# A hybrid transformer layer on one core: evacuations charged to the background steps' credit, the group norm's reciprocal root in three steps

## The chip, the cores and the metric

The kernel runs on one core of one Trainium2 chip. A core has a matrix engine (TensorE, PE in the profile), a vector engine (VectorE, DVE), an activation engine (ScalarE, ACT), a general engine (GpSimd, POOL) and a queue engine (SyncE, SP) that starts DMA transfers. Each engine works through its own list of instructions in order and waits on semaphores for the others. The metric is the time of one execution on the device in microseconds (us), the median of several runs.

## The reference

One layer of an encoder with three mixers side by side, then an MLP, for one sequence of 256 tokens with 2048 channels, all in float32. Cut to what matters here:

```python
u = rms_norm(x, norm_mix_pre)
proj = u @ w_in
sb, fox, rw, gates = split(proj)
y_a = stick_breaking_attention(sb)          # 4 heads x 128
y_b = forgetting_attention(fox)             # 4 heads x 128
y_c = rwkv7_time_mix(rw)                    # 16 heads x 64, 1024 channels
g_a, g_b, g_c = split(sigmoid(gates))       # 2048 channels each
m = g_a * (y_a @ w_branch_a) + g_b * (y_b @ w_branch_b) + g_c * (y_c @ w_branch_c)
x = x + rms_norm(m @ w_out, norm_mix_post)
x = x + rms_norm(square(relu(rms_norm(x, norm_mlp_pre) @ w_mlp_up)) @ w_mlp_down, norm_mlp_post)
```

The end of the RWKV mixer is a group norm over each head's 64 channels, and this is where the reciprocal root stands that the change takes apart:

```python
mean = jnp.mean(y, axis=-1, keepdims=True)
var = jnp.mean(jnp.square(y - mean), axis=-1, keepdims=True)
y = (y - mean) * rsqrt(var + 64e-5) * ln_w + ln_b
y = (y + sum(r * k * r_k) * v) * g
```

## The kernel before

**Weights as a stream.** All large weights are one stream of 128 x 1024 float32 tiles, read from memory in order into three buffers, `raw`. Each tile is split into two parts that together keep float32's precision: the high half `whi` (ScalarE, line L173) and the low half `wlo` (VectorE, L175, raw minus high). Three buffers of each exist, and the split runs one tile ahead of its use (`AHEAD` = 1). TensorE then needs, for each tile, eight matmuls of 512 columns with the high half and the equivalent of four with the low half. `gemm()` (L191, L195, L197) makes units of the first projections, `tok()` (L220, L235) computes token by channel and yields its two token tiles, whose product lies in a bank of PSUM, the buffer that matmuls write into.

**Mixers as background steps.** The small, latency-bound work of the three mixers runs between the large matmuls. It is one Python generator, `mixers()`: stick-breaking attention, forgetting attention, the RWKV's low-rank projections, then the RWKV mixer in two halves of eight heads, `rwkv_half(0)` and `rwkv_half(1)`. After each few large matmuls, `gemm()` and `tok()` call `tick(f)`. It adds `f * SHARE` to a credit, at most 1.5, counts a hold down by `f`, and while the hold is over and the credit is positive it takes steps from the generator:

```python
credit[0] = min(credit[0] + f * SHARE, 1.5)
hold[0] -= f
while hold[0] <= 0 and credit[0] > 0 and step():
    pass
```

`step()` subtracts from the credit what the step yielded. A plain number is a price. A `("stage", price, hold)` also ends the loop and sets the hold, so that the next step, which needs the result of this one, comes some large matmuls later. That fixes where the small matmuls stand on TensorE. The order on ScalarE, VectorE and GpSimd in this part of the kernel is chosen by the scheduler of the tile framework from the same program, by a model of its own; only TensorE keeps the written order there. From the first group of the output projection on, all engines keep the written order.

**The steps of one half of the RWKV mixer** that this text speaks of: the norm of the keys (L702 to L710), where ScalarE needs an activation table for Ln and another for Exp; `gates()` for each of four pairs of heads (L732 to L763), with the tanh gates on ScalarE, a scan along time on VectorE (L735), two exponentials on ScalarE that read it (L738, L739) and VectorE work that reads those (L744 to L763); four score matrices (L777 to L791); an inversion of triangular matrices by substitution on VectorE (L817 to L834), which ends in four 32 x 32 transposes and in matmuls of TensorE (L839); the recurrence over four chunks of 64 tokens, three stages each; and the group norm for two times two pairs (L917 to L946).

**The group norm** squares on ScalarE (L922), takes sums by matmul (L100, L101 in `heads()`), adds the epsilon on ScalarE (L935), and calls `rsqrt()` (L262): Ln and Exp(-0.5 x) on ScalarE, each with its table load (L265, L266), then one Newton step in four operations on VectorE (L267 to L270). All of it is one step of the generator, with a price of 2.2.

**The branches.** `branch()` (L1013) runs the products of the three mixers' outputs with their branch weights through `tok()`, for four groups of 512 channels. For each of the two token tiles VectorE evacuates PSUM: one operation for the first branch (L1017), two for the others (L1019, L1020). While the branches of the first two mixers run, `rwkv_half` is still taking steps.

Of the kernel before, what the change touches and what calls it, by code (L numbers as in the profile page):

```python
# [19 lines left out]
D = 2048  # L20
KT = 16
AHEAD = 1
SHARE = 0.82
HALF = 1024
EPS = 1e-6
CE = -0.5 * math.exp(-0.5)
# [26 lines left out]
def hybrid_block(ctx, tc, xt, x, gains, params, consts, lora, gup, wst, out):  # L53
# [12 lines left out]
    def nm(s):  # L66
        uid[0] += 1
        return f"{s}_{uid[0]}"
# [4 lines left out]
    def mps():  # L73
        return pm.tile([128, 512], F32, tag="mps", name=nm("mps"), bufs=4)
# [4 lines left out]
    def tmp(n=T):  # L79
        return tpool.tile([128, T], F32, tag="tmp", name=nm("tmp"), bufs=3)  # L80
# [5 lines left out]
    def C(name, r=slice(0, 128), lo=0, hi=None):  # L86
        c0, w = CC[name]
        hi = w if hi is None else hi
        if name == "ident":
            return ident[r, lo:hi]  # L90
        if c0 < NR + 128:
            return cr[r, c0 - 128 + lo:c0 - 128 + hi].bitcast(F32)
        return con[r, c0 - 128 - NR + lo:c0 - 128 - NR + hi]
# [17 lines left out]
    credit = [0.0]  # L111
# [25 lines left out]
    def tick(f=1.0):  # L137

        credit[0] = min(credit[0] + f * SHARE, 1.5)
        hold[0] -= f  # L140
# [119 lines left out]
            V.scalar_tensor_tensor(dst[:, T:], src, scale, dst[:, 0:T].bitcast(F32), ALU.mult, ALU.subtract)  # L260
            return ins

    def rsqrt(y, m, t):

        A.activation(t, m, AF.Ln)  # L265
        A.activation(y, t, AF.Exp, scale=-0.5)  # L266
        V.tensor_tensor(t, y, y, ALU.mult)  # L267
        V.tensor_tensor(t, t, m, ALU.mult)
        V.tensor_scalar(t, t, -0.5, 1.5, ALU.mult, ALU.add)
        V.tensor_tensor(y, y, t, ALU.mult)  # L270
# [6 lines left out]
    def g1(w=T):  # L277
        return rp.tile([128, T], F32, tag="g1", name=nm("g1"), bufs=21)
# [141 lines left out]
    rstd = rp.tile([128, T], F32, tag="cs", name="rstd1", bufs=1)  # L420
# [9 lines left out]
    def norm():  # L430
        ps = mps()
        for i in range(2):
            PE.matmul(ps[:, 0:T], C("ones"), A6[:, i, :], start=i == 0, stop=i == 1)
        ms, t = tmp(), tmp()
        V.tensor_scalar(ms, ps[:, 0:T], 1.0 / D, EPS, ALU.mult, ALU.add)
        rsqrt(rstd, ms, t)

    upk = [pk() for _ in range(KT)]

# [226 lines left out]
    def rwkv_half(hf):  # L666
# [30 lines left out]
        for i2, ps in enumerate(pss):  # L697
            ri = B6[:, 2 * i2:2 * i2 + 2, :]
            sc = B6[:, 4:6, :]
# [119 lines left out]
        for s in range(31):  # L819
            n, m = 31 - s, s + 1  # L820
# [35 lines left out]
        y = {p: g1() for p in PR}  # L856
# [55 lines left out]
        for i2 in range(2):  # L912
            gq = rp.tile([128, 3, 128], F32, tag="gup", name=nm("gup"), bufs=1)
            for i in range(2):
                cs = slice(128 * PR[2 * i2 + i], 128 * PR[2 * i2 + i] + 128)
                with tc.issue_after(behind[1].ins):
                    nc.scalar.dma_start(out=gq[:, i, :], in_=gup[0:128, cs])  # L917
                    nc.scalar.dma_start(out=gq[32 * i:32 * i + 32, 2, :], in_=gup[128:160, cs])
            B6 = rp.tile([128, 6, T], F32, tag="b6", name=nm("gn"), bufs=1)
            var, ri, sc = B6[:, 0:2, :], B6[:, 2:4, :], B6[:, 4:6, :]  # L920
            for i in range(2):
                A.activation(sc[:, i, :], y[PR[2 * i2 + i]], AF.Square)  # L922
            hi, lo = pair(), pair()
            A.activation(hi, sc, AF.Copy)
            V.tensor_tensor(lo, sc, hi.bitcast(F32), ALU.subtract)
            yield ("stage", 0.1, 2.5)
            ps = mps()
            heads(ps, hi, lo)
            psg = [mps(), mps()]
            for i in range(2):  # L930
                PE.matmul(psg[i][:, 0:T], gq[:, i, :], sy, start=True, stop=False)
            for i in range(2):
                r = slice(32 * i, 32 * i + 32)
                PE.matmul(psg[i][:, 0:T], gq[r, 2, :], sz[r], start=False, stop=True)
            A.activation(var, ps.rearrange("p (a b) -> p a b", a=2), AF.Identity, scale=1.0 / 64, bias=cst[:, 1:2])  # L935
            yield ("stage", 0.1, 0)
            rsqrt(ri, var, sc)
            yield 2.2
            for i in range(2):
                p = PR[2 * i2 + i]  # L940
                V.tensor_tensor(y[p], y[p], ri[:, i, :], ALU.mult)
                A.activation(y[p], y[p], AF.Identity, scale=P("lnw", p), bias=P("lnb", p))
                V.tensor_tensor(y[p], y[p], bon[p], ALU.add)
                V.tensor_tensor(y[p], psg[i][:, 0:T], y[p], ALU.mult)
                yc[p] = y[p]
                yield 1.1  # L946
# [22 lines left out]
    for br in ("sb", "fox"):  # L969
        for s in ("q", "k"):  # L970
# [3 lines left out]
            for h in range(4):  # L974
                ps = unit(upk)
                t = g1()
# [35 lines left out]
    def branch(ys, ths, m, first):  # L1012

        for tt, ps in enumerate(tok(ys)):
            th = ths[tt]
            if first:
                V.scalar_tensor_tensor(m[:, tt, :], th, 1.0, ps, ALU.add, ALU.mult)  # L1017
            else:
                V.scalar_tensor_tensor(th, th, 1.0, ps, ALU.add, ALU.mult)  # L1019
                V.tensor_tensor(m[:, tt, :], m[:, tt, :], th, ALU.add)  # L1020

    ms = []
    for g in range(4):
        m = rp.tile([128, 2, 512], F32, tag="m", name=nm("m"), bufs=4)
# [446 lines left out]
    first = [sum(SIZES[:q]) for q in range(len(SIZES) + 1)]  # L1471
# [178 lines left out]
```

## Time and profile before

| | us |
|---|---|
| median of three runs | 1511.27 |
| lowest and highest of them | 1511.23 and 1512.3 |
| the profiled execution | 1512.76 |
| its span, first to last instruction | 1510.9 |

The granted TensorE clock of the profiled execution is 0.998 of full speed.

In the profile's rows L12 is line 12 of the kernel. PE is a matmul on TensorE, PEld the load of its stationary operand. A row of the timeline gives start, duration, engine, line, operation, the tile written and the tile read, and how often; in square brackets stands how long the engine sat idle before it, and which instruction ended that. A row of the waits names who waited, for whom, the sum, how many times and the longest. A row of the windows gives the window, its length, the busy time of PE, PEld, DVE, ACT and POOL with the number of instructions, the granted clock, and the DMA engines' share and rate. A row of the chain of waits gives a start, a duration, an engine, a tile, a line and a count.

### The profile page before, as it was taken

What the parts mean: (1) busy time and instruction counts of PE and PEld (TensorE: products, weight loads), DVE (VectorE), ACT (ScalarE), POOL (GpSimd) and SP (SyncE); (2) the same over time, 40 slices, a digit from 0 to 9 for tenths busy, and PEclk for the clock granted to TensorE, in tenths of its full rate; (3) what the DMA queues carried; (4) which work ended last, traced back from release to release, by engine and by line L of the source; (5) the groups of instructions that cost most, each with busy time, mean ns of one, the idle gap of its engine ahead of it and who ended that gap; (6) DMA issues with size and microseconds to landing.
All of it is one profiled execution on the core that took longest, in us unless ns stands there. A gap on an engine that the chain in (4) does not pass through costs nothing.

```text
span 1510.9 us, 22695 instructions
## 1 busy us (share of the span) xinstructions
PE 1492.3 (99%) x8384; PEld 1252.7 (83%) x8384; DVE 1207.6 (80%) x1673; ACT 939.4 (62%) x1433; POOL 94.6 (6%) x151
## 2 busy tenths in 40 slices
PE   9999999999999999999999999999999999999997
PEld 7888888887787887778888988888888888888886
DVE  7875679895678896476656778999899989999996
ACT  7665677545676445564445767677667666766663
POOL 0031003000002000000000000000000000000000
PEclk9999999999999999999999999999999999999999
DMA  7645455455444455355675758879888888889874
GB/s 266 196 168 182 141 180 162 148 179 187 134 170 166 155 190 174 127 182 193 214 245 172 253 178 252 251 220 287 258 262 235 222 274 240 270 265 255 251 222 150
DMA packets 104687, 312.71 MB, mean 207 GB/s; under 512 B 10240, under 2 KB 12288, under 8 KB 104576
## 3 DMA queue, kind: packets, MB, share of 16 engines
q1 hardware_dynamic: 93968, 279.87, 55.1%
q0 software_dynamic: 8064, 29.36, 10.4%
q10 hardware_dynamic: 2544, 2.03, 0.5%
q8 instruction: 66, 1.08, 0.3%
q14 instruction: 45, 0.37, 0.1%
HBM read 279.77 MB, written 2.10 MB: 187 GB/s over the span
## 4 chain that ended last, share of the span: by engine, by line
PE 94%; DVE 2%; issue 1%; ACT 1%; DMA 1%; DVEq 0%; POOLq 0%; POOL 0%; ACTq 0%; SPq 0%
PE gps L235 26%; PE gps L191 23%; PE gps L195 13%; PE gps L220 7%; PE mps L1368 3%; PE mps L1370 3%; PE mps L1369 3%; PE gps L1370 2%; PE gps L1368 2%; PE gps L1369 2%; PE gps L197 2%; DVE wlo L175 1%; PE mps L777 1%; PE gps L1157 1%; DMA raw<-in_wst_dram 1%
## 5 line engine op out<-in xcount | busy, mean ns | idle before, releaser
L175 DVE TENSOR_TENSOR wlo<-raw,whi 128x1024 fp32r<-128x1024 f32 x576 | 697.0, 1220 | 160.5 <-ACT whi L173 149.2
L173 ACT ACTIVATE whi<-raw 128x1024 fp32r<-128x1024 f32 x576 | 603.9, 1057 | 251.9 <-PE gps L235 85.8
L191 PE MATMUL gps<-pk,whi 128*128 128x512 f32 x1479 | 375.3, 392 | 0.5 <-DVE tmp L1286 0.3
L191 PEld LDWEIGHTS gps<-pk,whi 128*128 128x128 f32 x1479 | 274.4, 188 | 56.1 <-ACT whi L173 0.9
L235 PE MATMUL gps<-whi,pk 128*128 128x512 f32 x1004 | 254.8, 393 | 1.4 <-ACT whi L173 1.3
L195 PEld LDWEIGHTS gps<-pk,wlo 128*128 128x128 f32 x1582 | 215.6, 190 | 15.2 <-DVE wlo L175 0.3
L235 PEld LDWEIGHTS gps<-whi,pk 128*128 128x128 f32 x1004 | 186.1, 188 | 42.6 <-ACT whi L173 2.2
L195 PE MATMUL gps<-pk,wlo 128*128 128x256 f32 x1582 | 221.0, 282 | 0.0
L235 PE MATMUL gps<-wlo,pk 128*128 128x512 f32 x502 | 137.8, 393 | 1.7 <-DVE wlo L175 1.7
L235 PEld LDWEIGHTS gps<-wlo,pk 128*128 128x128 f32 x502 | 93.2, 188 | 22.4 <-DVE wlo L175 2.9
L1368 PE MATMUL mps<-whi,fm 128*128 128x512 f32 x224 | 88.6, 396 | 1.9 <-ACT whi L173 1.7
L1285 ACT ACTIVATE tmp<-gps 128x256 f32<-128x256 f32 x64 | 24.6, 384 | 102.9 <-PE gps L197 101.0
L1369 PE MATMUL mps<-whi,fm 128*128 128x512 f32 x224 | 87.7, 392 | 0.0
L1370 PE MATMUL mps<-wlo,fm 128*128 128x512 f32 x224 | 87.4, 390 | 0.0
L1348 POOL DMA_DIRECT2D raw<-raw x56 | 48.8, 872 | 572.4 <-DVE raw L1345 271.9
L1345 DVE TENSOR_TENSOR raw<-raw,raw 128x1024 f32<-128x1024 f32 x56 | 68.4, 1221 | 0.8
L1368 PE MATMUL gps<-whi,fm 128*128 128x512 f32 x168 | 65.9, 392 | 0.0
L1370 PE MATMUL gps<-wlo,fm 128*128 128x512 f32 x168 | 65.8, 391 | 0.0
L1369 PE MATMUL gps<-whi,fm 128*128 128x512 f32 x168 | 65.5, 390 | 0.0
L220 PE MATMUL gps<-whi,pk 128*128 128x512 f32 x224 | 60.7, 393 | 0.0
L1368 PEld LDWEIGHTS mps<-whi,fm 128*128 128x128 f32 x224 | 42.4, 189 | 10.0 <-ACT whi L173 4.0
L1370 PEld LDWEIGHTS mps<-wlo,fm 128*128 128x128 f32 x224 | 42.1, 188 | 9.5
(346 smaller groups left out, 1725.1 us busy)
## 6 DMA issues: line engine op xcount, KB each, us to landing
raw<-in_wst_dram SPq DMA_DIRECT2D x516, 512.0 KB, 4.4
raw<-raw POOLq DMA_DIRECT2D x56, 512.0 KB, 7.3
x<-in_xt_dram SPq DMA_DIRECT2D x8, 256.0 KB, 6.8
x<-in_x_dram SPq DMA_DIRECT2D x8, 256.0 KB, 5.1
raw<-in_wst_dram SPq DMA_DIRECT2D x4, 256.0 KB, 4.8
g<-in_gains_dram SPq DMA_DIRECT2D x4, 256.0 KB, 5.0
pk<-in_gains_dram SPq DMA_DIRECT2D x4, 256.0 KB, 6.9
out_dram<-x SPq DMA_DIRECT2D x4, 256.0 KB, 2.8
```

The source lines that it names most:

```text
L173: A.activation(hi, raw, AF.Copy)
L175: low = lambda: V.tensor_tensor(lo, raw, hi.bitcast(F32), ALU.subtract)
L191: PE.matmul(ps, hi[:, i * 128:i * 128 + 128], pks[i], start=first and i == 0, stop=False)
L195: PE.matmul(ps[:, 0:T], lo[:, i * 128:i * 128 + 128], pks[i][:, 0:T], start=False, stop=False)
L197: PE.matmul(ps, hi[:, (n - 1) * 128:n * 128], pks[n - 1], start=False, stop=True)
L220: PE.matmul(ps[tt], pks[k][:, c:c + 128], w[:, (k - k0) * 512:(k - k0) * 512 + 512], start=k == 0 and part == 0 and w is hl[0], stop=w is ...
L235: PE.matmul(ps[tt], pks[k][:, c:c + 128], w[:, (k - k0) * 512:(k - k0) * 512 + 512], start=k == 0 and part == 0 and w is hl[0], stop=False)
L1345: V.tensor_tensor(R[d, a], R[d, a], R[d, b], ALU.add)
L1348: G.dma_start(out=R[d, a], in_=R[d, b], accum_op=ALU.add)
L1368: PE.matmul(Q[f], a, w, start=d == d0 and i == 0, stop=False)
L1369: PE.matmul(Q[f], b, w, start=False, stop=False)
L1370: PE.matmul(Q[f], a, wl, start=False, stop=d == dn and i == 1)
```

## The change

Three edits, all of which act on when the steps stand in the program.

- `SHARE`, the credit for a tick, goes from 0.82 to 0.88.
- `rsqrt()` is taken apart into a generator `power()` (Ln, a yield, Exp, a yield) and a function `newton()` (the four VectorE operations). The norm at the start of the kernel runs both through at once, as before. In the group norm each yield of `power()` becomes a stage with price 0.1 and hold 1, so that Ln, Exp and the Newton step are three steps.
- `branch()` subtracts 0.6 from the credit for a token tile of the first branch and 1.2 for one of the others, before its evacuation.

```diff
-SHARE = 0.82
+SHARE = 0.88
...
-    def rsqrt(y, m, t):
+    def power(y, m, t):
 
         A.activation(t, m, AF.Ln)
+        yield
         A.activation(y, t, AF.Exp, scale=-0.5)
+        yield
+
+    def newton(y, m, t):
+
         V.tensor_tensor(t, y, y, ALU.mult)
         V.tensor_tensor(t, t, m, ALU.mult)
         V.tensor_scalar(t, t, -0.5, 1.5, ALU.mult, ALU.add)
         V.tensor_tensor(y, y, t, ALU.mult)
...
-        rsqrt(rstd, ms, t)
+        for _ in power(rstd, ms, t):
+            pass
+        newton(rstd, ms, t)
...
             yield ("stage", 0.1, 0)
-            rsqrt(ri, var, sc)
+            for _ in power(ri, var, sc):
+                yield ("stage", 0.1, 1)
+            newton(ri, var, sc)
             yield 2.2
...
         for tt, ps in enumerate(tok(ys)):
             th = ths[tt]
+            credit[0] -= 0.6 if first else 1.2
             if first:
                 V.scalar_tensor_tensor(m[:, tt, :], th, 1.0, ps, ALU.add, ALU.mult)
             else:
```

The new lines move the numbers of the lines behind them: what was L702 to L763 is L709 to L770 in the changed kernel, L266 is L267, L942 is L951, L1008 is L1017, and L1019 and L1020 are L1029 and L1030. The numbers of instructions of each engine are the same before and after. Three places show how the order moves; the number at a row's start is its position in the engine's list, and the number behind a tile's name is its buffer's.

First ScalarE in the gate work of the first half, at about 229 us of the profile. Before:

```order
225 L702 ACT_TABLE_LOAD
226 L702 ACTIVATE b_376_2045<-sq_2185 128x512
227 L703 ACT_TABLE_LOAD
228 L703 ACTIVATE b_376_2045<-b_376_2045 128x512
229 L638 ACTIVATE tmp_2288<-gps_2210 128x256
230 L173 ACTIVATE whi_2332<-raw_2330 128x1024
231 L732 ACTIVATE lw_2274<-mps_2260,wah 128x256
232 L733 ACTIVATE tha_2276<-mps_2261,wah 128x256
233 L734 ACTIVATE lw_2274<-lw_2274,cst 128x256
234 L640 ACTIVATE zp_2290<-tmp_2289,par 128x256
235 L173 ACTIVATE whi_2369<-raw_2367 128x1024
236 L738 ACTIVATE ep_2278<-cs_2275 128x4x64
```

The same place in the changed kernel:

```order
225 L709 ACT_TABLE_LOAD
226 L709 ACTIVATE b_376_2045<-sq_2185 128x512
227 L710 ACT_TABLE_LOAD
228 L710 ACTIVATE b_376_2045<-b_376_2045 128x512
229 L739 ACTIVATE lw_2264<-mps_2250,wah 128x256
230 L740 ACTIVATE tha_2266<-mps_2251,wah 128x256
231 L741 ACTIVATE lw_2264<-lw_2264,cst 128x256
232 L750 ACTIVATE g_434_2287<-tha_2266,oka,wah 128x256
233 L645 ACTIVATE tmp_2299<-gps_2210 128x256
234 L745 ACTIVATE ep_2268<-cs_2265 128x4x64
235 L746 ACTIVATE em_2267<-cs_2265 128x256
236 L173 ACTIVATE whi_2332<-raw_2330 128x1024
```

The high half `whi_2332` stood two rows behind the table work and now stands behind the gate's four activations and behind both exponentials of the scan.

Then VectorE in the gate work of the second half, at about 460 us: `th` is the gate's tanh, `m` the sum of the branches, `wlo` a low half. Before:

```order
549 L735 SCALAR_TENSOR_TENSOR cs_4751<-con,lw_4750 128x256
550 L1019 SCALAR_TENSOR_TENSOR th_4695<-th_4695,gps_4705 128x512
551 L175 TENSOR_TENSOR wlo_4771<-raw_4768,whi_4770 128x1024
552 L1020 TENSOR_TENSOR m_4201<-m_4201,th_4695 128x512
553 L1019 SCALAR_TENSOR_TENSOR th_4703<-th_4703,gps_4706 128x512
554 L744 TENSOR_TENSOR g_916_4778<-g_916_4778,g_538_2736 128x256
555 L1020 TENSOR_TENSOR m_4201<-m_4201,th_4703 128x512
556 L747 SCALAR_TENSOR_TENSOR tha_4752<-tha_4752,em_4753 128x256
557 L754 TENSOR_TENSOR At_4784<-g_916_4778,em_4753 128x4x64
558 L752 SCALAR_TENSOR_TENSOR At_4784<-kkr_4781,tha_4752 128x4x64
559 L175 TENSOR_TENSOR wlo_4800<-raw_4797,whi_4799 128x1024
560 L175 TENSOR_TENSOR wlo_4818<-raw_4815,whi_4817 128x1024
```

In the changed kernel:

```order
549 L753 SCALAR_TENSOR_TENSOR kkr_4758<-g_542_2747,par,b_836_4442 128x256
550 L751 TENSOR_TENSOR g_910_4755<-g_910_4755,g_542_2747 128x256
551 L754 SCALAR_TENSOR_TENSOR tha_4732<-tha_4732,em_4733 128x256
552 L761 TENSOR_TENSOR At_4761<-g_910_4755,em_4733 128x4x64
553 L759 SCALAR_TENSOR_TENSOR At_4761<-kkr_4758,tha_4732 128x4x64
554 L1029 SCALAR_TENSOR_TENSOR th_4695<-th_4695,gps_4710 128x512
555 L175 TENSOR_TENSOR wlo_4782<-raw_4779,whi_4781 128x1024
556 L1030 TENSOR_TENSOR m_4225<-m_4225,th_4695 128x512
557 L1029 SCALAR_TENSOR_TENSOR th_4708<-th_4708,gps_4711 128x512
558 L175 TENSOR_TENSOR wlo_4800<-raw_4797,whi_4799 128x1024
559 L1030 TENSOR_TENSOR m_4225<-m_4225,th_4708 128x512
560 L175 TENSOR_TENSOR wlo_4818<-raw_4815,whi_4817 128x1024
```

Ahead of the low half `wlo_4800` stand two operations since the one before it, and not seven; the pair's gate work has moved ahead of the low half before.

Last ScalarE at the end of the second half, between the first and the second pair of the group norm, at about 640 us. Before, from the row behind the norm's Exp and its next high half on:

```order
601 L1008 ACTIVATE th_6497<-gps_6211 128x512
602 L1008 ACTIVATE th_6512<-gps_6212 128x512
603 L917 DMA gup_6532<-in_gup_dram 128x128
604 L942 ACTIVATE g_1138_5977<-g_1138_5977,par 128x256
605 L942 ACTIVATE g_1139_5978<-g_1139_5978,par 128x256
606 L918 DMA gup_6532<-in_gup_dram 32x128
607 L922 ACTIVATE gn_6537<-g_1140_5979 128x256
608 L256 ACTIVATE pk_6494<-g_1138_5977 128x256
609 L922 ACTIVATE gn_6537<-g_1141_5980 128x256
610 L256 ACTIVATE pk_6509<-g_1139_5978 128x256
611 L924 ACTIVATE hl_6540<-gn_6537 128x512
612 L173 ACTIVATE whi_6548<-raw_6546 128x1024
```

In the changed kernel, from the norm's Ln on:

```order
598 L265 ACT_TABLE_LOAD
599 L265 ACTIVATE gn_6447<-gn_6447 128x512
600 L924 DMA gup_6586<-in_gup_dram 128x128
601 L267 ACT_TABLE_LOAD
602 L267 ACTIVATE gn_6447<-gn_6447 128x512
603 L173 ACTIVATE whi_6540<-raw_6538 128x1024
604 L925 DMA gup_6586<-in_gup_dram 32x128
605 L924 DMA gup_6586<-in_gup_dram 128x128
606 L925 DMA gup_6586<-in_gup_dram 32x128
607 L173 ACTIVATE whi_6572<-raw_6570 128x1024
608 L173 ACTIVATE whi_6602<-raw_6600 128x1024
609 L951 ACTIVATE g_1141_6003<-g_1141_6003,par 128x256
```

Ln and Exp still follow each other, with the issue of a DMA between. Behind them stand three high halves, and then L951 (before: L942) with the rest of the norm, where one stood before. The matmuls L839 (now L846) of the first half's inversion stand 30 large matmuls earlier on TensorE, and the four transposes ahead of them have no low half between them any more.

## The prediction

> **What bounds the kernel now.** First the page: how busy each engine is, and the chain that ended last.
>
> ```profile
> PE 1492.3 (99%) x8384; PEld 1252.7 (83%) x8384; DVE 1207.6 (80%) x1673; ACT 939.4 (62%) x1433; POOL 94.6 (6%) x151
> PE 94%; DVE 2%; issue 1%; ACT 1%; DMA 1%; DVEq 0%; POOLq 0%; POOL 0%; ACTq 0%; SPq 0%
> ```
>
> TensorE (PE) has work in 1492.3 of 1510.9 us, and the chain of waits runs through it for 94%. The change leaves the number of matmuls as it is, so it can move the time only through the 18.6 us in which PE stands still, or by adding to them. The mixers run from about 190 to 650 us, so next come the windows in which PE is idle there, and all its waits between 190 and 810 us.
>
> ```profile
> 450.00:500.00 50.00, 48.29 (x237) 38.75 (x237) 41.12 (x61) 30.03 (x48) 10.06 (x16) 1.00 0.50 164
> 550.00:600.00 50.00, 49.77 (x393) 39.64 (x393) 37.26 (x59) 24.66 (x41) 0.00 (x0) 1.00 0.56 185
> 600.00:650.00 50.00, 48.66 (x435) 38.15 (x435) 26.69 (x46) 30.23 (x62) 0.00 (x0) 1.00 0.36 119
> PE gps L235 <- DVE wlo L175: 1.7, 1, 1.7
> PE gps L235 <- ACT whi L173: 1.3, 1, 1.3
> PE gps L220 <- DVE wlo L175: 0.2, 1, 0.2
> ```
>
> The first column behind the window is its length, the second PE's busy time: 1.71, 0.23 and 1.34 us are missing, at full clock (1.00). The waits name the same three stalls: twice a low weight half that VectorE (DVE) made too late, once a high half from ScalarE (ACT). So the most that this change can win by mending is about 3.6 us (below), 0.24% of the time; everything else in it can only add. A gap's cost is counted from one start to the next, because a pipelined matmul's last tail hides in the gap. The rate comes from a stretch without a stall in the chain of waits:
>
> ```profile
> 56.46 19.06 PE gps L235 x84
> ```
>
> 19.06 / 84 = 0.227 us for a matmul.
>
> **The change part by part.** It adds no instruction: the three pieces of the reciprocal root are the same Ln, Exp and four DVE operations, and the charge to the credit is arithmetic while the program is written. Its direct cost is zero. What it does is move steps: with SHARE at 0.88 for 0.82 the first half's steps stand 6 big matmuls earlier at its start and about 30 earlier at its end, and the second half's, charged for the branches' evacuations, 4 earlier at first and some 20 to 36 later at the end. Four places then matter.
>
> *C, gate work of the second half, around 464 us (PE, then DVE).*
>
> ```profile
> 462.10 1.98 PE L235 MATMUL gps<-whi,pk 128*128 128x512 f32 x8
> 465.79 1.20 PE L235 MATMUL gps<-wlo,pk 128*128 128x512 f32 x4 [1.71 <-DVE wlo L175]
> ```
>
> ```profile
> 460.83 0.68 DVE L1020 TENSOR_TENSOR m<-m,th 128x512 f32<-128x512 f32 x1
> 461.43 0.68 DVE L1019 SCALAR_TENSOR_TENSOR th<-th,gps 128x512 f32<-128x512 f32 x1
> ...
> 462.42 1.17 DVE L1020 TENSOR_TENSOR m<-m,th 128x512 f32<-128x512 f32 x1
> 463.51 0.41 DVE L747 SCALAR_TENSOR_TENSOR tha<-tha,em 128x256 f32<-128x256 f32 x1
> ...
> 464.19 0.41 DVE L752 SCALAR_TENSOR_TENSOR At<-kkr,tha 128x256 f32<-128x256 f32 x1
> 464.52 2.34 DVE L175 TENSOR_TENSOR wlo<-raw,whi 128x1024 fp32r<-128x1024 f32 x2
> ```
>
> The eight matmuls should have handed over at 462.10 + 8 x 0.227 = 463.91; the next start at 465.79: 1.88 us lost. Between 460.83 and 464.52 DVE ran 3.69 us of branch evacuations (L1019, L1020) and gate work (L744 to L752) ahead of the split PE wanted. In the changed order the gate work stands one split earlier and the last L1020 one split later: of the row's seven operations two stay between those two splits, 0.68 + 0.68 = 1.36 us, less than the 12 matmuls (2.72 us) of a weight tile. But the split before it now has the gate work and the first L1019 ahead of it, so a rest of the delay may move to that one: 0.3 us, bounds 0 and 0.9 (half of the stall). Gain 1.6.
>
> *D, last group norm, around 648 us (ACT, then PE).*
>
> ```profile
> 636.08 1.28 ACT L265 ACT_TABLE_LOAD   x1
> 637.37 0.63 ACT L265 ACTIVATE gn<-gn 128x512 f32<-128x512 f32 x1
> 638.02 1.28 ACT L266 ACT_TABLE_LOAD   x1
> 639.32 0.63 ACT L266 ACTIVATE gn<-gn 128x512 f32<-128x512 f32 x1
> 639.85 1.04 ACT L173 ACTIVATE whi<-raw 128x1024 fp32r<-128x1024 f32 x1
> ...
> 644.09 0.60 ACT L942 ACTIVATE g<-g,par 128x256 f32<-128x256 f32 x1 [1.87 <-DVE g L941]
> ...
> 647.28 2.94 ACT L173 ACTIVATE whi<-raw 128x1024 fp32r<-128x1024 f32 x3
> ```
>
> ```profile
> 645.96 1.07 PE L235 MATMUL gps<-wlo,pk 128*128 128x512 f32 x4
> 648.37 1.21 PE L235 MATMUL gps<-whi,pk 128*128 128x512 f32 x4 [1.34 <-ACT whi L173]
> ```
>
> Here 648.37 - (645.96 + 4 x 0.227) = 1.50 us are lost. From 636.08 to 639.95 ACT is in the root's two table loads and two activations; after one split (639.85) it takes the norm's next pieces, with 1.87 us idle for DVE ahead of L942, and comes to the next split at 647.28. In the changed order Ln and Exp still follow one another on ACT, with a DMA issue between them only, so the split in three steps changes nothing inside the block. But directly behind it now stand three high halves, and only then L942's successors: the wait for DVE comes after the weights, not ahead of them. Three tiles are 3 x 12 x 0.227 = 8.2 us of matmuls, against the 6.4 us from the end of the split at 640.89 to the next at 647.28. Gain 1.5, bounds 0 and 1.5. The DMA issues of the norm's weights move ahead with it, in the same number.
>
> A rule bears on this place. The Trainium skill ("ScalarE: Activation LUTs", section "Table sets: the hidden batching unit") says to batch activations by table set, since a switch costs time; a yield between Ln and Exp invites a foreign function in between and with it another load. Its section "What ACT_TABLE_LOAD costs" prices a switch at 1283 ns plus a drain of about 1380 ns. The trace agrees with the first (636.08, 1.28) and not with the second: Ln starts at 637.37, 0.01 us after the load's end. The order of the change holds as many loads as before, 23, so by the rule the sum keeps its value; by the page's price one load more would be 2.66 us on ACT, by the row 1.28.
>
> The small stall of 0.2 us at 571 us (third waits row) stands behind a pair of transposes and a split on DVE that the later second half moves away; gain 0.2, bounds 0 and 0.2.
>
> *A, gate work of the first half, around 229 us.* Before, a high half (L173) stands on ACT ahead of the gate work L732 to L739; in the change it stands behind it, and behind L738 and L739, which wait for DVE's scan L735.
>
> ```profile
> 224.51 1.05 ACT L173 ACTIVATE whi<-raw 128x1024 fp32r<-128x1024 f32 x1
> ...
> 453.24 0.40 ACT L739 ACTIVATE em<-cs 128x256 f32<-128x256 f32 x1
> ```
>
> ```profile
> 224.38 0.43 DVE L705 TENSOR_SCALAR b<-b 128x512 f32<-128x512 f32 x1 [1.11 <-ACT b L703]
> ...
> 449.21 0.43 DVE L705 TENSOR_SCALAR b<-b 128x512 f32<-128x512 f32 x1 [0.99 <-ACT b L703]
> ...
> 452.20 0.68 DVE L735 TENSOR_TENSOR_SCAN cs<-con,lw 128x256 f32<-128x256 f32 x1
> ```
>
> ```profile
> 229.10 2.00 PE L191 MATMUL gps<-pk,whi 128*128 128x512 f32 x8
> ```
>
> The chain L705, 706, 708, 709, 710, 735, 738, 739 that the change makes there without a split in between is the one that the second half ran at 449 us: from L705's start to L739's end 453.64 - 449.21 = 4.43 us. Begun at 224.38 it ends at 228.81, and the high half, 1.05 us, overlapping by 0.1, at 229.76. PE wants it at 229.10: 0.66 us late. Its low half on DVE then waits for three gate operations (1.0 us in place C, 463.51 to 464.52) and takes 1.22 (half of 2.34, rounded up): 228.81 + 1.0 + 1.2 = 231.0, against 229.76 + 8 x 0.227 = 231.6, in time; if these three run at twice the time it is 0.4 late. I take 0.9, bounds 0.5 and 1.4 (below 0.5 only if ACT comes to the block earlier, which nothing here lets it do).
>
> *B, the inversion of the first half, around 338 us.* In the change the 64 small matmuls of L839 stand on PE directly behind four low-half matmuls, the place where PE was at 337.45, and not at 344.64; they need all four transposes L829 and L834 on DVE, which now run without a split between them.
>
> ```profile
> 281.37 0.42 DVE L639 TENSOR_TENSOR tmp<-gps,tmp 128x256 f32<-128x256 f32 x1 [2.25 <-ACT tmp L638]
> 282.32 1.23 DVE L175 TENSOR_TENSOR wlo<-raw,whi 128x1024 fp32r<-128x1024 f32 x1 [0.53 <-ACT whi L173]
> ...
> 335.15 2.18 DVE L829 STREAM_TRANSPOSE TW<-Ti 32x512 f32<-32x512 f32 x2
> 337.23 1.05 DVE L834 STREAM_TRANSPOSE SC<-Ti 32x512 f32<-32x512 f32 x1
> ...
> 339.37 1.09 DVE L834 STREAM_TRANSPOSE SC<-Ti 32x512 f32<-32x512 f32 x1
> ```
>
> ```profile
> 337.45 1.97 PE L235 MATMUL gps<-whi,pk 128*128 128x512 f32 x8
> ...
> 344.64 0.75 PE L839 MATMUL mps<-TW,SC 32*32 32x32 f32 x64
> ```
>
> The transposes are 2.18 + 1.05 + 1.09 = 4.32 us. From 282.32 to 341 DVE knows no pause, so they can begin before 335.15 only by as much of the 2.25 + 0.53 = 2.78 us of idle time ahead of that stretch as the earlier steps fill. Half of it, 1.4, lets them end at 335.15 - 1.4 + 4.32 = 338.07, 0.6 us behind PE's 337.45. None of it: 1.9 (with 0.1 of overlap); all: nothing. I take 0.6, nearer to the filled end because the steps come 1.4 us (6 matmuls) earlier from the first half's start on. What is late next is the split behind the transposes, whose use, eight matmuls and L839's 0.75 later, leaves it 1 us to spare.
>
> The rest of the two halves, with other edits at nothing: each evacuation and split keeps its engine and its duration, POOL's steps that move along meet an engine that is busy for 6% of the span, SP's weight loads keep their order, PE shows no wait but the three above there, and the credit's changed totals give their steps back within the same branches. 0, bounds -0.5 and +0.6. From wo's first group on, the order is that of the program, and the end's chain is the same.
>
> **The sum**, for the profiled execution of 1512.76 us (span 1510.9, 1.86 us lie around it): -1.6 (C) - 1.5 (D) - 0.2 + 0.9 (A) + 0.6 (B) = -1.8 us. That execution stands 1.49 us above the median of the three runs, 1511.27, and what I forecast is the median: 1511.27 - 1.8 = 1509.5 us. With all costs at their lower bounds and the gains whole it is -3.6 + 0.5 - 0.5 = -3.6, 1507.7; with C's rest at 0.9, D's gain gone, A, B and the rest at the upper ends it is -1.0 + 1.4 + 1.9 + 0.6 = +2.9, 1514.2. The likeliest case's own range, not all at one end at once, is 1508.0 to 1512.0.
>
> **The rivals.** A measurement of this kernel can tell about 0.2% from no change, 3.0 us: below 1508.2 it is faster, above 1514.3 slower.
>
> *The stalls go and nothing takes their place.* The waits at A and B are covered, because ACT reaches the gate work earlier and DVE fills its idle time. For it: the steps do come earlier as a whole, and idle time is there (1.13 to 2.25 us at a piece before 282 us). Against it: at A the chain starts from the same table load, behind the same split. -3.6 and perhaps 0.5 of small gaps: 1507.4.
>
> *The group norm's stall stays.* Since Ln and Exp remain neighbours on ACT, the split in steps may do nothing, and a high half may still be late behind L942 and the norm's next pieces. Against it the order: three halves ahead. The sum loses 1.5: 1511.0.
>
> *Slower: the recurrence comes too close.* Each half runs four chunks of three stages, 24 in all, in which PE waits for ACT and DVE copies of the stage before. With more credit the stages follow one another sooner, and a copy that then stands behind a low split (1.22) holds PE. It decides from a mean of (3.0 + 1.8) / 24 = 0.2 us a stage on; at 0.3 it is +7.2 - 1.8, 1516.7. For it: DVE has no pause for 50 us in the first half. Against it: before, none of these stages shows as a wait of PE, and the minimum distance of a stage is a count of ticks, which SHARE doesn't touch.
>
> **How the numbers follow.** The forecast has 0.52, the full gain 0.26, the stall that stays 0.09, the recurrence 0.13. The forecast reaches below 1508.2 with 0.06 of its chance and the slower case is the only one much above 1514.3 (0.01 of the forecast's upper tail joins it): faster 0.32, same 0.54, slower 0.14. The range runs from 1507.0, below the full gain, to 1513.3, which leaves most of the recurrence case and a little on each side out, about 2 in 10.
>
> **What would show it.** In the profile of the changed kernel the waits of PE should no longer hold 1.7 on a low half near 464 nor 1.3 on a high half near 648, or only a rest of some tenths. New ones should stand near 230 us on the high half of L173 (0.6 to 0.7) and near 338 us at the matmuls of the inversion, on the transposes (about 0.6). PE's busy time stays 1492 us. If the new waits are absent, the first rival holds; if waits of some tenths stand in a row between 345 and 450 or from 580 to 640 us, the recurrence decides. Wrong from the ground up would be a changed idle time of PE behind 660 us, where I let the change move nothing.

## The result, and the profile after

| | before | with the change |
|---|---|---|
| median of 12 runs each, us | 1511.94 | 1509.01 |
| lowest and highest | 1510.82 to 1514.18 | 1506.92 to 1511.34 |
| span of the profiled execution | 1510.9 | 1507.6 |

The ratio is 0.9979, with a 95% interval of 0.9972 to 0.9986: 3.2 us (2.1 to 4.2) faster, at the edge of what was called measurable. The forecast was 1.8 us (1509.5), with a range of 1507.0 to 1513.3.

The page of the changed kernel, busy time:

```profile
PE 1492.0 (99%) x8384; PEld 1254.0 (83%) x8384; DVE 1206.6 (80%) x1673; ACT 939.8 (62%) x1433; POOL 94.5 (6%) x151
```

The work is the same; only the time without work is shorter. Its windows, in the order and columns of those shown of before, and then all its waits of PE between 190 and 810 us:

```profile
450.00:500.00 50.00, 49.94 (x251) 40.58 (x250) 40.74 (x58) 28.18 (x45) 8.95 (x16) 1.00 0.55 178
550.00:600.00 50.00, 50.00 (x393) 40.27 (x392) 38.57 (x62) 24.84 (x39) 0.00 (x0) 1.00 0.62 192
600.00:650.00 50.00, 50.00 (x443) 39.41 (x442) 25.77 (x42) 29.84 (x60) 0.00 (x0) 1.00 0.42 136
```

```profile
PE gps L191 <- ACT whi L173: 0.5, 1, 0.5
```

The three waits of before are gone and one new one has come, in the place and of the kind that was forecast at A. The one forecast at B is not there. To see where each part of a microsecond went, the large matmuls (those with weights from the stream) are numbered in the order of their starts. Their sequence is the same in both kernels, and the small ones move between them, so the difference between the starts of the same large matmul is the kernel's lead or lag at that point. The table takes numbers at which neither kernel has a step under way that the other has not.

| large matmul | start before, us | start after, us | shift, us | what lies between |
|---|---|---|---|---|
| 1060 | 224.43 | 224.32 | -0.11 | |
| 1185 | 248.03 | 249.08 | +1.05 | A |
| 1930 | 427.52 | 427.91 | +0.39 | B and the rest of the first half |
| 2300 | 526.85 | 525.22 | -1.63 | C |
| 2730 | 643.69 | 641.57 | -2.12 | the small stall at 571 us |
| 2880 | 681.54 | 677.75 | -3.79 | D |
| last | 1500.95 | 1497.67 | -3.28 | output projection and MLP |

The mixers' stretch is 3.79 us shorter. Behind it, the shift goes to -2.04 us at 1110 us and back to -3.61 at 1228 us: the two executions differ there by single waits of PE in the MLP, before by one of 1.1 us for a high half, after by one of 1.0 us for VectorE (L1296). The experiments below are therefore read by their shift at large matmul 2880, behind the mixers, next to the ratio of their times. Each shift is that of one execution: at large matmul 1060, ahead of A, the shifts of all twelve kernels lie between -0.35 and +0.21 us, so a few tenths between two kernels mean little.

Place A in the changed kernel: ScalarE, then VectorE's low half, then PE.

```profile
225.73 0.37 ACT L645 ACTIVATE tmp<-gps 128x256 f32<-128x256 f32 x1
227.95 0.42 ACT L745 ACTIVATE ep<-cs 128x256 f32<-128x256 f32 x1 [1.85 <-DVE cs L742]
228.28 0.40 ACT L746 ACTIVATE em<-cs 128x256 f32<-128x256 f32 x1
228.58 1.04 ACT L173 ACTIVATE whi<-raw 128x1024 fp32r<-128x1024 f32 x1
```

```profile
229.47 0.90 DVE L761 TENSOR_TENSOR At<-g,em 128x256 f32<-128x256 f32 x1
230.29 0.41 DVE L759 SCALAR_TENSOR_TENSOR At<-kkr,tha 128x256 f32<-128x256 f32 x1
230.63 1.21 DVE L175 TENSOR_TENSOR wlo<-raw,whi 128x1024 fp32r<-128x1024 f32 x1
```

```profile
228.75 0.39 PE L197 MATMUL gps<-pk,whi 128*128 128x512 f32 x1
229.68 2.11 PE L191 MATMUL gps<-pk,whi 128*128 128x512 f32 x8 [0.54 <-ACT whi L173]
231.89 1.22 PE L195 MATMUL gps<-pk,wlo 128*128 128x256 f32 x8
```

ScalarE stands still for 1.85 us ahead of L745, with the weights' split queued behind it, and PE's eight matmuls start at 229.68. The low half ends at 231.84, and PE's next group starts at 231.89: it is late too, by about 0.4 us against eight matmuls of 0.227.

Place C: VectorE, then PE.

```profile
459.59 0.68 DVE L1029 SCALAR_TENSOR_TENSOR th<-th,gps 128x512 f32<-128x512 f32 x1
460.19 1.22 DVE L175 TENSOR_TENSOR wlo<-raw,whi 128x1024 fp32r<-128x1024 f32 x1
461.32 0.68 DVE L1030 TENSOR_TENSOR m<-m,th 128x512 f32<-128x512 f32 x1
461.93 0.68 DVE L1029 SCALAR_TENSOR_TENSOR th<-th,gps 128x512 f32<-128x512 f32 x1
462.52 1.22 DVE L175 TENSOR_TENSOR wlo<-raw,whi 128x1024 fp32r<-128x1024 f32 x1
```

```profile
461.46 1.20 PE L235 MATMUL gps<-wlo,pk 128*128 128x512 f32 x4
462.49 1.98 PE L235 MATMUL gps<-whi,pk 128*128 128x512 f32 x8
464.31 1.07 PE L235 MATMUL gps<-wlo,pk 128*128 128x512 f32 x4
```

The low half that came 1.88 us late before is made 0.57 us ahead of its use (463.74 to 464.31); the one before it (460.19 to 461.41) is used at 461.46, late by 0.2 us against eight matmuls of 0.227 from 459.42.

Place D: ScalarE behind the norm's Exp, then PE.

```profile
642.24 0.63 ACT L267 ACTIVATE gn<-gn 128x512 f32<-128x512 f32 x1
642.78 1.05 ACT L173 ACTIVATE whi<-raw 128x1024 fp32r<-128x1024 f32 x1
644.03 1.06 ACT L173 ACTIVATE whi<-raw 128x1024 fp32r<-128x1024 f32 x1 [0.21 <-PE gps L235]
646.75 1.07 ACT L173 ACTIVATE whi<-raw 128x1024 fp32r<-128x1024 f32 x1 [1.66 <-PE gps L235]
648.03 1.09 ACT L951 ACTIVATE g<-g,par 128x256 f32<-128x256 f32 x2 [0.21 <-DVE g L950]
```

```profile
646.55 1.07 PE L235 MATMUL gps<-wlo,pk 128*128 128x512 f32 x4
647.46 1.98 PE L235 MATMUL gps<-whi,pk 128*128 128x512 f32 x8
```

Now ScalarE waits for PE to free a weight buffer (1.66 us), not PE for ScalarE, and L951 comes behind the weights.

### The profile page after: what moved, and what is told of

Its sections match the earlier page's. It is cut to its first block, busy times and chain, and to the rows that moved or that the text cites. A ratio compares the mean times of both kernels' runs of the same rounds, so it can differ in the third digit from the quotient of the medians.

```text
span 1507.6 us, 22703 instructions
## 1 busy us (share of the span) xinstructions
PE 1492.0 (99%) x8384; PEld 1254.0 (83%) x8384; DVE 1206.6 (80%) x1673; ACT 939.8 (62%) x1433; POOL 94.5 (6%) x151
## 4 chain that ended last, share of the span: by engine, by line
PE 89%; DMA 4%; DVE 2%; issue 2%; ACT 2%; POOLq 0%; SPq 0%; DVEq 0%; POOL 0%; ACTq 0%
PE gps L235 27%; PE gps L191 21%; PE gps L195 12%; PE gps L220 7%; PE mps L1378 3%; PE mps L1380 3%; PE mps L1379 3%; DMA raw<-in_wst_dram 2%; PE gps L1380 2%; PE gps L1378 2%; PE gps L1379 2%; DMA raw<-raw 2%; PE gps L197 1%; DVE wlo L175 1%; ACT whi L173 1%
```

## The experiments

Eleven kernels were run, each timed against the kernel before on the same chip. All results in one table; the shift is that of large matmul 2880 in the profiled execution against the kernel before's 681.54 us. The intervals of the ratios from 0.9976 to 0.9986 overlap, so between those kernels only the traces can show a difference.

| run | SHARE | charge | root in steps | shift, us | ratio of times (95%) |
|---|---|---|---|---|---|
| the change | 0.88 | yes | 3 | -3.79 | 0.9979 (0.9972 to 0.9986) |
| share first 0.82, then 0.88 | 0.82/0.88 | yes | 3 | -2.98 | 0.9986 (0.9977 to 0.9994) |
| no split | 0.88 | yes | 1 | -2.73 | 0.9986 (0.9977 to 0.9994) |
| share alone | 0.88 | no | 1 | -0.12 | 0.9997 (0.9989 to 1.0006) |
| split alone | 0.82 | no | 3 | +0.03 | 1.0002 (0.9993 to 1.0011) |
| charge alone | 0.82 | yes | 1 | +9.14 | 1.0068 (1.0055 to 1.0082) |
| no charge | 0.88 | no | 3 | -3.79 | 0.9977 (0.9968 to 0.9986) |
| no share | 0.82 | yes | 3 | +9.09 | 1.0063 (1.0051 to 1.0075) |
| first share and hold | 0.82/0.88 | yes | 3 | -3.66 | 0.9976 (0.9968 to 0.9985) |
| share 0.84 | 0.84 | yes | 3 | +4.93 | 1.0048 (1.0035 to 1.0061) |
| share 0.92 | 0.92 | yes | 3 | +0.76 | 1.0012 (1.0003 to 1.0021) |
| share 0.96 | 0.96 | yes | 3 | -1.40 | 1.0000 (0.9991 to 1.0009) |

**What does place A cost?** The old credit until 72 weight tiles are split, then the new one:

```diff
-        credit[0] = min(credit[0] + f * SHARE, 1.5)
+        credit[0] = min(credit[0] + f * (SHARE if uid2[0] > 72 else 0.82), 1.5)
...
     def wsplit(raw, n=None, now=True):
+        uid2[0] += 1
```

> The change with the old credit of 0.82 for the first 72 weight tiles and 0.88 from then on. The order keeps the high half ahead of the first half's gate work on ScalarE, as before the change, and has the whole second half as in the change. My theory (place A costs the change 1.05 us, the shift between the two profiles at 229 us, and nothing else depends on it): PE's wait on the high half at about 229 us is gone, and the kernel is 1.0 us faster than the change, about 4.2 us (0.28%) under the kernel before, with a shift of -4.5 to -5 us against it at 660 us. Rival (the time lost at A is won back in the idle time of what follows): the shift at 660 us stays at -3.8 us and the time that of the change.

The wait at 229 us is gone (large matmul 1185 starts at 248.16, +0.13), and yet the kernel is not faster than the change: its shift is 0.81 us worse. The time comes back at place B. VectorE, then PE, of this kernel (its lines are two further on: L177 is the low half, L843 the transposes into SC, L237 the matmuls):

```profile
335.17 2.18 DVE L838 STREAM_TRANSPOSE TW<-Ti 32x512 f32<-32x512 f32 x2
337.25 2.14 DVE L843 STREAM_TRANSPOSE SC<-Ti 32x512 f32<-32x512 f32 x2
339.42 3.50 DVE L177 TENSOR_TENSOR wlo<-raw,whi 128x1024 fp32r<-128x1024 f32 x3
```

```profile
337.54 1.98 PE L237 MATMUL gps<-whi,pk 128*128 128x512 f32 x8
340.70 0.73 PE L237 MATMUL gps<-wlo,pk 128*128 128x512 f32 x2 [1.19 <-DVE wlo L177]
```

Here the transposes begin at 335.17, where the forecast had its upper bound (335.15), and the low half behind them is 1.2 us late. The same place in the change, VectorE, then PE:

```profile
334.58 2.17 DVE L836 STREAM_TRANSPOSE TW<-Ti 32x512 f32<-32x512 f32 x2
336.65 2.12 DVE L841 STREAM_TRANSPOSE SC<-Ti 32x512 f32<-32x512 f32 x2
```

```profile
337.56 1.07 PE L235 MATMUL gps<-wlo,pk 128*128 128x512 f32 x4
338.55 0.75 PE L846 MATMUL mps<-TW,SC 32*32 32x32 f32 x64
```

VectorE is 0.6 us earlier there, and PE, which lost 1.05 us at A, comes 0.9 us later: its four low-half matmuls from 337.56 are started by 338.47, where the other kernel stands at 337.54. So both theories were wrong in the time: with the wait at A gone, one of the same size stands at B, and in the change the delay from A can cover it. A's delay is not the only difference, though. Here the small matmuls (L848) stand ten large matmuls later than in the change, so that their 0.7 us don't lie ahead of the low half that PE waits for.

**What does the split in three steps do?** The root in one step again:

```diff
             for _ in power(ri, var, sc):
-                yield ("stage", 0.1, 1)
+                pass
             newton(ri, var, sc)
```

> The change with the group norm's root in one step again (SHARE 0.88 and the charge stay). The order puts the last norm's Ln, Exp and tail on ScalarE between the same weight tiles as before the change. Theory (the split mends the stall of 1.50 us at 648 us because its holds move the norm's tail behind three high halves): the stall at the last norm is back with about 1.5 us, shift at 660 us -2.3 us, time 1.7 us under the kernel before. Rival (the split does nothing, the earlier steps of SHARE mend it): no stall, shift -3.8 us as in the change.

The longer of PE's two waits in this kernel, 190 to 810 us (the other is the 0.5 us at A):

```profile
PE gps L235 <- ACT whi L173: 1.3, 1, 1.3
```

The stall at the last norm is back with the size that it had before, as the theory has it; the shift is -2.73 and not -2.3, since at large matmul 2300, behind place C, this kernel is 0.5 us ahead of the change. With the other two edits beside it the split is worth about 1.1 us in the traces, the two shifts' difference; the two times, 0.9986 and 0.9979, don't tell it apart from nothing.

**Each edit alone.** SHARE alone (the other two undone):

> SHARE 0.88 alone, no charge and no split. Theory (a stall arises where a lump of the steps falls between two splits and its place decides, whatever the edit is meant for): place A costs 1.05 us as in the change, the stall at 464 us is gone because the gate work stands several splits earlier than the evacuations, the norm's table loads and its tail fall between different tiles so that its stall goes too; shift at 660 us -2.5 to -4 us. Rival (each edit mends what it is meant for: the charge the evacuations at 464 us, the split the norm at 648 us): both stalls stay, and with A's cost the shift is about +0.5 us.

The stalls at 464 and 648 us are gone without the edits that were made for them, as the theory has it, and yet the shift is -0.12 for the theory's -2.5 to -4. The waits of this kernel between 400 and 640 us say why, with VectorE's and PE's rows at the first of them behind it:

```profile
PE mps L101 <- DVE hl L932: 2.3, 2, 1.3
```

```profile
407.07 0.42 DVE L952 TENSOR_TENSOR g<-g,g 128x256 f32<-128x256 f32 x1
407.40 0.69 DVE L932 TENSOR_TENSOR hl<-gn,hl 128x512 fp32r<-128x512 f32 x1
```

```profile
408.14 0.51 PE L101 MATMUL mps<-hl,cr 128*128 128x512 f32 x1 [1.30 <-DVE hl L932]
```

The second pair's sums (L101) wait for a low half of its squares (L932), which VectorE makes behind the first pair's tail (L950 to L953) and two weight splits. Neither theory had this wait. With the charge or the split beside it, it does not occur.

The split alone (SHARE 0.82, no charge):

> The split in three steps alone, SHARE 0.82 and no charge. Theory (places decide): A's cost is absent; the norm's stall is gone (-1.5 us); the norm of the first half with its new holds moves the second half's gate work later, onto the evacuations at 464 us, 11 us of VectorE work and splits within the two tiles there (5.4 us of matmuls), so that the stall at this place grows from 1.9 to some 2.5 to 4 us; shift at 660 us -1 to +1 us. Rival (the split mends the norm alone): shift at 660 us -1.5 us, the stall at 464 us stays at 1.9 us.

The shift is +0.03. PE's waits at 440 to 480 us:

```profile
PE gps L235 <- DVE wlo L175: 2.5, 2, 2.3
```

As forecast the norm's stall goes and the one at 464 us grows, from 1.7 to 2.5 us of wait: the holds of the first half's norms have pushed the second half's gate work onto the evacuations. Another 1.1 us go in a wait for a low half at 579 us, which neither theory had.

The charge alone:

> The charge for the branches' evacuations alone (SHARE 0.82, root in one step). Its first half is that of before, so neither place A nor B costs anything; on VectorE ten operations stand between two splits at 464 us; the last norm's matmuls stand at the end of the stretch of 2816 large matmuls, behind which the loop takes all steps that are left without matmuls between. Theory (places decide): the stall at 464 us stays or grows (2 to 4 us), and the last norm is partly exposed at about 670 us; slower than before by 1 to 6 us. Rival (the charge mends the evacuations at 464 us): that stall is gone, 2 us faster than before.

It is 0.68% slower, 10.3 us, more than either theory gave (and the stall at 464 us, 1.2 us of wait, less than the theory's). PE waits for the sums of the last norm, here in the waits between 190 and 720 us, and the window's idle time and clock are the two numbers to read in the row behind (43.59 of 50 us busy, clock 0.90):

```profile
PE mps L100 <- ACT hl L931: 3.8, 1, 3.8
```

```profile
650.00:700.00 50.00, 43.59 (x169) 33.20 (x168) 30.65 (x46) 26.97 (x36) 0.00 (x0) 0.90 0.40 129
```

**Each edit left out.** Without the charge:

> SHARE 0.88 and the root in three steps, without the charge. Theory (places decide): A costs 1.0 us, the stalls at 464 and 648 us are gone since the gate work and the norm stand at other tiles, but, as with SHARE alone, the sums of the second norm wait for VectorE behind the first norm's tail (1.0 and 1.3 us with SHARE alone); shift at 660 us -0.5 to -2.5 us, short of the change's -3.8. Rival (the charge adds nothing to the other two): shift as in the change, -3.8 us.

The rival holds: -3.79 us, the same as the change, and no wait on the norm's sums. Beside the other two the charge is worth nothing that can be measured. Without the higher SHARE:

> The charge and the root in three steps with SHARE at 0.82. The order has both last norms' matmuls at large matmul 2816, where the loop drains what is left. Theory (0.88 pays for the credit and the holds that the other two edits take; without it the last norms fall behind the last large matmul that could hide them): two norms of some 8 us from sums to product, of which the three tiles of the following branch hide part: PE idle for 5 to 15 us at 660 to 690 us, time 5 to 15 us over the kernel before. Rival (SHARE only brings A's loss): 3 to 5 us faster than before.

The theory holds: 0.63% slower, 9.5 us, in the middle of its range of 5 to 15. PE's waits at 650 to 700 us, and two windows of that time:

```profile
PE mps L100 <- ACT hl L931: 9.4, 1, 9.4
PE gps L220 <- DVE pk L257: 0.9, 1, 0.9
```

```profile
665.00:670.00 5.00, 0.00 (x0) 0.00 (x0) 4.41 (x9) 1.94 (x5) 0.00 (x0) 0.50 0.02 4
670.00:675.00 5.00, 4.30 (x11) 2.52 (x12) 1.69 (x4) 3.58 (x7) 0.00 (x0) 0.58 0.00 0
```

Credit and holds that the charge and the split take make the steps late; behind the gate products of the third branch, `while not fin[0]: step()` takes what is left with no large matmul between (the drain, from here on), and PE waits 9.4 us. None of the three edits alone gains anything (shifts of -0.12, +0.03 and +9.14 us); SHARE with the split gives the whole gain.

**A mended version.** The first experiment with a longer hold behind the first three of the four transposes into SC:

```diff
-                yield ("stage", 1.0, 0.5 + 3 * b * (c.start > 0))
+                yield ("stage", 1.0, (1.2 if hf == 0 and not (b and c.start) else 0.5) + 3 * b * (c.start > 0))
```

> The first experiment (0.82 for the first 72 tiles, 0.88 behind them) with a hold of 1.2 for 0.5 after the first three of the four transposes of the inversion's second kind in the first half, so that a low half stands between them on VectorE, as before the change, and the matmuls behind them 12 large matmuls later. The second half moves with it by 12 to 24 matmuls. Theory (what A's delay hid in the change was the wait at B of 1.2 us that the first experiment showed; with a split between the transposes it goes): no wait at 229 nor at 340 us, shift at 430 us about 0 for the change's +0.4 and the first experiment's +1.2; with the stalls at 464 and 648 us gone as in the change, shift at 660 us -4 to -5 us and time 1.0 us under that of the change. Rival (each mended place leaves its debt to the next): a new wait between 340 and 470 us or at the last norm, which now ends 3 tiles ahead of the drain, takes it back, shift at 660 us -3.5 us or less.

No wait at 229 nor at 340 us, and still -3.66 us. Large matmul 1645 starts at 341.31 (0.29 us ahead of before), 1930 at 428.06 (0.54 behind it): 0.8 us went between 341 and 428 us. The shift lies between the two ranges, but the loss stands where the rival has it. PE's only waits between 190 and 720 us:

```profile
PE mps L855 <- ACT TW L851: 0.5, 3, 0.2
```

They stand at 348 us, among the next matmuls of the inversion (L855), which read ScalarE's copies (L851) of the results of those at B. They begin 5.1 us behind those at B, and began 6.4 us behind them before the change. From their first start to that of the next large matmul it takes 1.83 us, 0.69 before the change. The kernel's ratio, 0.9976, can't be told from the change's 0.9979, nor from 0.9977 without the charge.

**Other values of SHARE**, with the charge and the split as in the change:

> The change with SHARE at 0.84 for 0.88. The order has the second norm of the last half at large matmul 2816, in the drain, the first at 2772. Theory (a drained norm costs PE's idle time, below some value of SHARE the change turns slower): one norm exposed as with the charge alone, +9 us at 660 to 690 us, in all 6 to 9 us slower than before. Rival (the change's gain comes from SHARE by degrees): between the kernel before and the change, -1 to -3 us.

> The change with SHARE at 0.92. The norms stand at 2676 and 2742, far from the drain; in the first half VectorE has the end of the inversion and its four transposes, 14 operations, between two splits. Theory (no value between 0.86 and 0.96 is better as such; the places that happen to fall together decide): the stalls at 464 and 648 us are gone, A is smaller, a new stall of 1 to 3 us stands at 320 to 335 us; shift at 660 us -1.5 to -3.5 us. Rival (more credit is better): shift -4 us or more.

> The change with SHARE at 0.96. The norms stand at 2604 and 2670; VectorE has 11 operations with the four transposes between two splits, one less wide than at 0.92, and the second half's gate work stands well ahead of 464 us. Theory (places decide): a stall of 0.5 to 2 us near 325 us, the others gone, and smaller ones where a split and a lump meet in the second half's scores; shift at 660 us -1.5 to -4 us. Rival (steps that come too close hold PE at each stage of the recurrence): waits at many stages, slower than before.

0.84 falls into the drain and is 7 us slower (0.48%), as the theory has it, though its shift of +4.93 is short of the +9. It also bears on places A and B: like the first experiment it has no wait at 229 us, and one of 1.2 us for the low half behind the four transposes, at 340 us; its small matmuls stand 16 large matmuls later than in the change. At 0.92 and 0.96 the new stall stands where the lump of transposes was read in the order, 2.7 and 2.2 us of idle time in the timelines of PE, the first row 0.92's, the second 0.96's:

```profile
335.33 1.20 PE L235 MATMUL gps<-wlo,pk 128*128 128x512 f32 x4 [2.73 <-DVE wlo L175]
```

```profile
330.05 0.75 PE L846 MATMUL mps<-TW,SC 32*32 32x32 f32 x64 [2.16 <-DVE TW L836]
```

At 0.96 the shift, -1.40, is just outside the theory's range, and the stall just above it. At 0.92 the shift is far above the range (+0.76 for -1.5 to -3.5), though the stall has the forecast size. One reason is that A is not smaller: in both kernels PE waits 0.9 us there, now for the low half. This is 0.92's row:

```profile
231.97 1.21 PE L195 MATMUL gps<-pk,wlo 128*128 128x256 f32 x8 [0.87 <-DVE wlo L175]
```

The other is that behind the new stall PE was also slow. The next full group of 0.92 on PE, and the window it lies in:

```profile
337.32 3.41 PE L235 MATMUL gps<-whi,pk 128*128 128x512 f32 x8
```

```profile
338.00:340.00 2.00, 2.00 (x6) 1.57 (x5) 0.00 (x0) 0.44 (x1) 0.00 (x0) 0.50 0.71 272
```

Eight matmuls take 3.41 us, elsewhere 1.98, at a clock of 0.50: 1.4 us more. More credit is not better, and in neither kernel is there a row of waits along the recurrence.

## Why the prediction was right, point by point

**What bounds the kernel** held: the three waits of PE that were read between 190 and 660 us were the ones that went. Behind 660 us, where a changed idle time was to count as a sign of being wrong, this pair differs by +0.5 us on the whole, by single waits in the MLP.

**D**, -1.5 forecast: from -2.12 to -3.79 it is -1.67, and the split is what does it beside the charge (without it 1.3 us of wait return). How it does it was read rightly: Ln and Exp remain neighbours, and the hold puts the weights ahead of L951.

**C**, -1.6 forecast (-1.9 with a rest of 0.3): -2.02, the rest was 0.2. Not the charge as such does it: SHARE alone and SHARE with the split have no stall of its size there either, the charge alone has one of 1.2 us there. What counts, as far as these orders show, is that gate work and evacuations don't meet between two splits.

**The stall at 571 us**, -0.2: -0.49. Counted from one start to the next, as the other two were, it would have been larger than the idle time that was used.

**A**, +0.9: +1.16, from the mechanism named: the chain to L746 ends at 228.68 (forecast 228.81), the high half comes 0.7 us later than PE wants it (229.68 for 228.75 + 0.227) and the low half another 0.4.

**B and the rest of the first half**, +0.6 and 0: together -0.66. This is the step that failed, in two terms. B cost nothing in the change: its small matmuls start at 338.55, and the four ahead of them are started by 338.47. The forecast added B to A as if the two were independent, but how late VectorE is at B counts from where PE stands, and PE was 0.9 us late from A. In the two kernels with the four transposes in one lump and no wait at A (the first experiment and 0.84), PE waits 1.2 us at B, between the forecast's 0.6 and its upper bound of 1.9. Since the small matmuls stand later in both, it is not shown that the delay from A alone makes the difference. The transposes begin 0.57 us earlier than before (334.58 for 335.15), where the forecast had 1.4. The rest, put at nothing, is the other term: it gained 0.66 us. Some 0.55 of that are large matmuls that start 0.1 to 0.2 us later than their usual distance from the one before (0.227 us for 512 columns), too little for the list of waits: 22 of them between 1185 and 1930 before, 18 with the change. The largest, 0.2 us at 426.95 before the change, waited for a high half.

The sum was thus 1.9 us short in the mixers' stretch: 1.2 from B and the rest, 0.4 from C, 0.3 and 0.2 from the small stall and D, less 0.3 from A. Behind the mixers +0.5 us in this pair of executions gives part of it back.

That the forecast of 1509.5 lies so close to the measured 1509.0 is in part luck: the three runs from which it was reckoned had a median 0.7 us below that of the twelve, and against the measured 3.2 us the forecast of 1.8 us was 1.4 short.

**The rivals.** "The stalls go and nothing takes their place" gave 1507.4, 3.9 us; the time came out between it and the forecast, and its reason is half true (no wait at B, but one at A). "The norm's stall stays" is what the kernel without the split shows, not the change. The recurrence cost nothing in the change; the slower outcome that does exist in these edits is another one, the drain, which the prediction didn't have. At 0.84 for 0.88 the same change is 7 us slower. The order shows it beforehand, as the number of the large matmul behind which the last norm stands: 2784 of 2816 in the change, 2816 at 0.84.

## What to carry to other kernels

When background steps are laid between the matmuls by a budget, a stall is made by the place where two lumps meet between two splits, not by the total: read the order lump by lump and price each against the matmuls it must hide behind, and see first that no step falls behind the last large matmul. Delays in such a chain don't add: mend one and ask whether a later place had been covered by it. A constant that wins by 0.2% here (0.88) loses at 0.84 and 0.92, so it must be looked for again after every other edit.

## What the runs showed of the hardware

A wait of PE can cost more than its length, since the granted clock can fall to half around it. Without the higher SHARE, with 9.4 us of idle time up to 670.67, it is 0.50 at 665 to 670 us, 0.58 at 670 to 675 and 1.00 from 675 on. At SHARE 0.92 a wait of 2.73 us is enough: 0.50 at 338 to 340 us, some 3 us after the wait's end, and 1.4 us lost.

The length of the wait alone doesn't decide. Two shorter ones did it too: one of 2.0 us at SHARE 0.84, with 0.2 us more right behind it (clock 0.93 at 650 to 700 us), and one of 2.09 us in the MLP of the first experiment, behind which seven matmuls take 3.36 us:

```profile
PE mps L100 <- ACT hl L931: 2.0, 1, 2.0
650.00:700.00 50.00, 46.44 (x188) 35.81 (x187) 32.81 (x48) 29.04 (x37) 0.00 (x0) 0.93 0.45 148
```

```profile
1213.98 3.36 PE L193 MATMUL gps<-pk,whi 128*128 128x512 f32 x7 [2.09 <-ACT whi L175]
```

Yet the wait of 2.16 us at 0.96, the one of 2.26 us with the split alone and the one of 1.71 us before the change left the clock at 1.00 in their windows. In the traces the half clock comes in stretches of 3.41 us, or of two or three times that: 336.76 to 340.17 at 0.92, 1213.93 to 1217.35 in the first experiment, 665.59 to 672.41 at 0.84, 663.98 to 674.22 without the higher SHARE. What decides beside the length was not tested.

The Trainium skill ("TensorE: Matmul & The Clock Gate", section "What's actually happening") has PE fall to half its clock after an idle window of about 3.4 us. The runs agree in the half, and differ in the length of the wait: 2.73, 2.09 and 2.0 us each did it once.
